# An encoder layer on one core: four of seven product sums moved into PSUM, operand pages freed one by one, second norm's statistics on ScalarE

## The chip, the cores and the metric

The kernel runs on one core of a Trainium2 chip. The metric is the device time of one execution in microseconds. The kernel before takes 1025.63 us (median of 3 runs, 1025.45 to 1026.38).

## The reference, cut to what matters

One layer of an encoder on 512 tokens of width 1024, in float32:

```
x = layer_norm(alpha*x + 0.5*swiglu_1(x))              # width 2816 in between
h = x @ w_in                                           # one projection, split into attention and conv parts
mix = concat([sparse_attention(h), short_conv(h)]) @ w_out
x = layer_norm(alpha*x + mix)                          # "second norm"
x = layer_norm(alpha*x + 0.5*swiglu_2(x))
x = x + sigmoid(x @ ple_gate_w) * (p @ ple_proj_w)     # "gate" and "embed"

swiglu(x, wg, wu, wd) = (silu(x @ wg) * (x @ wu)) @ wd
layer_norm(x) = (x - mean) * rsqrt(var + eps) * g + b  # over the 1024 columns of a token
```

## The kernel before, in words

The 512 tokens stand as four blocks of 128 (`nat[t]`), and transposed as operands. Every float32 matrix product is made of three passes on TensorE: an operand is split into a hi part (a cast on ScalarE, L111) and a lo part (a subtraction on VectorE, L112), and hi*hi, hi*lo and lo*hi are summed in PSUM (`mm`, L132). A recording layer with priorities sets the order of the instructions on each engine; each engine, and SP's queue of DMA issues, then works through its own list in that order.

On-chip memory is 38 pages of 4 KB per partition, handed out by `page` from a first-in first-out list and given back by `free`; the next user of a page waits for the last user of the one before. A load (`unit`, L114) takes three pages: raw, hi and lo, and gives raw back. PSUM has eight banks; `bank("all")` goes round them.

`ffn` (L244) goes through the 22 chunks of 128 of the middle width in groups of 4, 4, 4, 4 and 6. The first two chunks are plain products (`plain`). The other 20 go in ten pairs (`two`, L309): a pair of chunks by two halves of the tokens by two halves of the 1024 rows is a 2 by 2 block product, done with seven products in place of eight. `weights` (L276) loads the two halves of a pair's columns of wg or wu and makes the operands A11, A12/A22, S1/S2 and S3/S4 of them by additions on VectorE (L293, L294, L299, L300) and splits; `Quarters` makes the operands B and T of the tokens. One product is 2 matrices (g and u) x 4 x 3 = 24 matmuls of 256 columns, g in the left half of a bank and u in the right. Each product has a bank of its own, and `two` adds them up outside PSUM: one copy on ScalarE (L340), seven additions on VectorE (L341, 342, 344, 345, 347, 348, 349), into pages `e` (two) and `k` (two). `put_chunk` (L332) does silu on ScalarE (L336), the multiplication on VectorE (L337) and the split of the result. All of a pair's operand pages, `e` and `k` are given back at its end (L351). After each group comes the down projection (96 matmuls of 512 columns for four chunks) with the wd units, which are loaded as pages and priority allow; in the last group it goes block by block, with the layer norm (`ln_tb`, L156: aggregate L158, pow on GpSimd L160, two passes on VectorE L161 and L162) and the transposes (L146) of each block behind it.

Ahead of the second norm (L749 to L763) the output projection of block t is added to `nat[t]` (L757), `bn_stats` takes statistics on VectorE (L758), `ln_tb` follows, and `Quarters.block` transposes the block (L201), casts hi (L204), subtracts lo (L205) and copies raw (L224). The products `p @ ple_proj_w` (`embed`, L425) are made during the attention and around the second norm as filling work, copied to four pages (`prj`, L433) and held there until the gate at the very end (L785). The attention keeps its softmax rows in a ring of two tiles of 1280 columns (L686).

## Time and profile before

| | |
|---|---|
| median of 3 runs | 1025.63 us (1025.45 to 1026.38) |
| the profiled execution | 1025.29 us |
| its span | 1023.4 us |
| TensorE busy | 1004.4 us, 98% of the span |
| VectorE, ScalarE busy | 823.5 us (80%), 442.6 us (43%) |
| stages by the span | first feed-forward to about 330 us, first norm and combined projection, attention to about 600, second norm to about 630, second feed-forward to about 970, third norm and gate to the end |

The profiled execution takes 1.9 us more than its span, which lie before the first and behind the last instruction. An engine's busy time says how much of the span it worked; what it waited for stands in the timeline in square brackets, as the idle time just before an instruction and the instruction that released it. A wait of TensorE delays the end where TensorE has no idle time left to make up for it.

### The profile page before, as it was taken

How to read it: one execution, taken by the hardware profiler on the slowest of the kernel's cores; microseconds unless marked ns; L12 is line 12 of the kernel's file. 1: busy time of each engine (PE TensorE's matmuls, PEld its weight loads, DVE VectorE, ACT ScalarE, POOL GpSimd, SP SyncE). 2: the span in 40 equal slices, each digit the busy share in tenths (PEclk: the TensorE clock that was granted, in tenths of full speed). 3: DMA queues.
4: the chain of work that ended last, by engine and by line, in shares of the span. 5: the costliest groups of instructions: out<-in, count | busy, mean ns of one | idle time of the engine just before them, and what ended most of it. 6: DMA issues, size and time to landing. Idle time of an engine off the chain costs nothing.

```text
span 1023.4 us, 15531 instructions
## 1 busy us (share of the span) xinstructions
PE 1004.4 (98%) x6311; PEld 902.3 (88%) x6311; DVE 823.5 (80%) x1289; ACT 442.6 (43%) x627; POOL 27.0 (3%) x35
## 2 busy tenths in 40 slices
PE   9999999999999989999999999999999999999998
PEld 7989999898998868888878788989999898998787
DVE  7997868978698946999679988896868969698952
ACT  7544334433355225432576736443425324246221
POOL 1000000000002100000000011000000000000100
PEclk9999999999999999999999999999999999999999
DMA  9532324323226322423112222431324322236111
GB/s 306 162 109 83 104 83 145 101 80 113 79 100 200 83 61 62 120 67 84 61 42 103 83 71 94 128 120 45 120 84 144 103 79 89 82 124 226 56 38 51
DMA packets 99606, 104.57 MB, mean 102 GB/s; under 512 B 5968, under 2 KB 82000, under 8 KB 99536
## 3 DMA queue, kind: packets, MB, share of 16 engines
q1 hardware_dynamic: 99536, 103.60, 32.0%
q8 instruction: 49, 0.80, 0.3%
q14 instruction: 21, 0.17, 0.1%
HBM read 101.49 MB, written 2.10 MB: 101 GB/s over the span
## 4 chain that ended last, share of the span: by engine, by line
PE 87%; DVE 4%; DMA 4%; ACT 3%; issue 1%; SPq 1%; POOL 0%; POOLq 0%; ACTq 0%; DVEq 0%
PE bk L132 84%; DVE pg L112 2%; ACT pg L111 2%; DMA pg<-in_ffn_wd_dram 1%; PE bk L524 1%; DMA pg<-in_ffn_wu_dram 1%; PE bk L525 1%; PE bk L722 1%; PE bk L146 1%; DMA pg<-in_x_t_dram 1%; DMA pg<-in_ple_proj_w_dram 1%; ACT a L694 0%; SPq L214 0%; DMA pg<-in_ple_gate_w_dram 0%; DVE nat L162 0%
## 5 line engine op out<-in xcount | busy, mean ns | idle before, releaser
L132 PE MATMUL bk<-pg,pg 128*128 128x256 f32 (+1 forms) x2832 | 496.7, 333 | 4.9 <-DVE pg L112 2.1
L132 PEld LDWEIGHTS bk<-pg,pg 128*128 128x128 f32 x2832 | 427.3, 190 | 57.2 <-DVE pg L112 3.9
L111 ACT CAST pg<-pg 128x1024 fp32r<-128x1024 f32 (+1 forms) x270 | 260.0, 976 | 303.3 <-PE bk L132 76.0
L112 DVE TENSOR_TENSOR pg<-pg,pg 128x1024 fp32r<-128x1024 f32 (+1 forms) x270 | 301.1, 1126 | 38.3 <-ACT pg L111 33.0
L132 PE MATMUL bk<-xq,pg 128*128 128x256 f32 x2208 | 274.7, 284 | 2.2 <-DVE mv L158 1.4
L132 PEld LDWEIGHTS bk<-xq,pg 128*128 128x128 f32 x2208 | 269.4, 192 | 5.9 <-ACT pg L433 1.8
L132 PE MATMUL bk<-xT,pg 128*128 128x512 f32 (+2 forms) x600 | 133.0, 381 | 0.2 <-ACT xT L111 0.2
L132 PEld LDWEIGHTS bk<-xT,pg 128*128 128x128 f32 (+1 forms) x600 | 110.1, 186 | 21.2 <-ACT xT L111 0.5
L132 PE MATMUL bk<-pg,xT 128*128 128x512 f32 (+1 forms) x312 | 69.8, 374 | 2.0 <-DVE nat L394 1.7
L132 PEld LDWEIGHTS bk<-pg,xT 128*128 128x128 f32 x312 | 54.9, 188 | 12.2 <-ACT pg L111 2.1
L336 ACT ACTIVATE a<-pg 128x512 f32<-128x512 f32 x40 | 25.2, 630 | 78.0 <-DVE pg L345 70.8
L111 ACT CAST pg<-hf 128x512 fp32r<-128x512 f32 (+1 forms) x56 | 34.6, 618 | 37.6 <-DVE hf L337 19.3
L112 DVE TENSOR_TENSOR pg<-hf,pg 128x512 fp32r<-128x512 f32 (+1 forms) x56 | 38.7, 690 | 4.1 <-ACT pg L111 3.8
L408 DVE SCALAR_TENSOR_TENSOR nat<-bk,nat 128x512 f32<-128x512 f32 x64 | 40.3, 682 | 1.2 <-PE bk L132 1.2
L345 DVE TENSOR_TENSOR pg<-bk,pg 128x512 f32<-128x512 f32 x20 | 13.8, 691 | 29.3 <-PE bk L132 29.0
L337 DVE TENSOR_TENSOR hf<-a,pg 128x512 f32<-128x512 f32 x40 | 27.5, 688 | 11.8 <-ACT a L336 11.7
L160 POOL TENSOR_TENSOR mv<-mv,mhalf 128x1 f32<-128x1 f32 x12 | 17.8, 1479 | 630.4 <-DVE mv L159 630.4
L112 DVE TENSOR_TENSOR pg<-bk,pg 128x512 fp32r<-128x512 f32 (+2 forms) x37 | 22.5, 626 | 12.8 <-ACT pg L111 12.4
L293 DVE TENSOR_TENSOR pg<-pg,pg 128x512 f32<-128x512 f32 x40 | 27.3, 686 | 5.6 <-DMA pg<-in_ffn_wg_dram 5.0
L299 DVE TENSOR_TENSOR pg<-pg 128x512 f32<-128x512 f32 x40 | 27.4, 685 | 2.5 <-PE bk L132 2.5
L294 DVE TENSOR_TENSOR pg<-pg,pg 128x512 f32<-128x512 f32 x40 | 27.4, 684 | 0.0
L300 DVE TENSOR_TENSOR pg<-pg,pg 128x512 f32<-128x512 f32 x40 | 27.0, 685 | 0.1
(100 smaller groups left out, 614.5 us busy)
## 6 DMA issues: line engine op xcount, KB each, us to landing
pg<-in_ffn_wd_dram SPq DMA_DIRECT2D x44, 512.0 KB, 4.0
pg<-in_ffn_wu_dram SPq DMA_DIRECT2D x43, 512.0 KB, 4.8
pg<-in_ffn_wg_dram SPq DMA_DIRECT2D x43, 512.0 KB, 3.9
pg<-in_w_in_dram SPq DMA_DIRECT2D x28, 512.0 KB, 3.6
pg<-in_w_out_dram SPq DMA_DIRECT2D x8, 512.0 KB, 3.9
pg<-in_ple_gate_w_dram SPq DMA_DIRECT2D x8, 512.0 KB, 3.7
pg<-in_x_t_dram SPq DMA_DIRECT2D x8, 256.0 KB, 5.8
nat<-in_x_dram SPq DMA_DIRECT2D x4, 512.0 KB, 9.2
```

The costliest lines, as they stand in the source:

```text
L111: nc.scalar.copy(hi, src)
L112: nc.vector.tensor_sub(lo, src, hi.bitcast(F32))
L132: nc.tensor.matmul(ps, lhsT=st[a], rhs=mv[b], start=first and i == 0 and k == 0, stop=last and i == n - 1 and k == 2)
L160: nc.gpsimd.tensor_tensor(mv[:, 3:4], mv[:, 2:3], mhalf, op=ALU.pow)
L293: nc.vector.tensor_add(S1, A21, A22)
L294: nc.vector.tensor_sub(S2, S1, A11)
L299: nc.vector.tensor_sub(S3, A11, A21)
L300: nc.vector.tensor_sub(S4, A12, S2)
L336: nc.scalar.activation(s_t, e[m][:, :, 0], AF.Silu)
L337: nc.vector.tensor_mul(h3, s_t, e[m][:, :, 1])
L345: nc.vector.tensor_add(e[0][:, 1], prod("S4", "B22"), u4)
L408: nc.vector.scalar_tensor_tensor(dst, acc[t], CY, dst, op0=ALU.mult, op1=ALU.add)
```

## The change

It has these parts:

- In `two`, the seven products are taken in another order, and partial sums are kept in PSUM: A11B11, S2T2, S3T3 and A22T4 follow each other in one bank (`x_`), S1T1 and S4B22 in a second (`y_`), A12B21 has a third. The running sums are read out between: four copies on ScalarE (L365, 366, 367, 372) and three additions on VectorE (L368, 369, 370). The pages `k` are gone.
- In `weights`, the operands are made in the order in which the products take them (A11, S1/S2, S3/S4, A12/A22), and each operand's pages are given back with the last product that uses them; the pages of `e` are given back in `put_chunk` (L360).
- 40 pages in place of 38. The first warm-up tile lies in `nat[0]`.
- `prj` is stored to DRAM when it is made (L458) and loaded again for the gate (4 x 512 KB each way, on SP's queue).
- The softmax rows of a head lie in two pages (768 and 512 columns) in place of the ring.
- In the second norm, blocks 0 to 2 take their statistics on ScalarE: a pass for the sum, one for the sum of squares, each with an accumulator (`ln_tb_act`). Block 3 keeps `bn_stats`.

```diff
-NPAGES = 38
-WSTEPS = (1, 2, 1)
+NPAGES = 40
...
+    def ln_tb_act(r, g, b):
+        mv, junk = ring("mv", 4, [P, 4]), page([P, D], F32)
+        nc.scalar.activation(junk, r, AF.Identity, accum_out=mv[:, 0:1])
+        nc.vector.tensor_scalar(mv[:, 0:1], mv[:, 0:1], -1.0 / D, None, op0=ALU.mult)
+        nc.scalar.activation(junk, r, AF.Square, bias=mv[:, 0:1], accum_out=mv[:, 1:2])
+        free(junk)
+        nc.vector.tensor_scalar(mv[:, 2:3], mv[:, 1:2], 1.0 / D, LN_EPS / ALPHA ** 2, op0=ALU.mult, op1=ALU.add)
+        nc.gpsimd.tensor_tensor(mv[:, 3:4], mv[:, 2:3], mhalf, op=ALU.pow)
+        nc.vector.scalar_tensor_tensor(r, r, mv[:, 0:1], g, op0=ALU.add, op1=ALU.mult)
+        nc.vector.scalar_tensor_tensor(r, r, mv[:, 3:4], b, op0=ALU.mult, op1=ALU.add)
...
-            pages += [a11, *a2, *h12, *h34]
+            ops["S3"], ops["S4"] = (ops["S3"], h34), (ops["S4"], [])
+            yield
+            a2 = page([P, 4, 2 * P]), page([P, 4, 2 * P])
+            split(*a2, r[1])
+            free(r[1])
+            ops["A12"], ops["A22"] = (tuple(z[:, :, m * P:(m + 1) * P] for z in a2) for m in range(2))
+            ops["A12"], ops["A22"] = (ops["A12"], []), (ops["A22"], a2)
             yield
...
-            def prod(a, b):
-                ps = bank("all").rearrange("p (m n) -> p m n", m=2)
+            def product(ps, a, b, first):
                 for i, (nm, _) in enumerate(mats):
-                    mm(ps[:, i], [((W[nm][a][0][:, c], W[nm][a][1][:, c]), (X.q[b][0][:, c], X.q[b][1][:, c])) for c in range(4)])
+                    w = W[nm][a][0]
+                    for c in range(4):
+                        for k, (x_, y_) in enumerate(PASSES):
+                            nc.tensor.matmul(ps[:, i], lhsT=w[x_][:, c], rhs=X.q[b][y_][:, c],
+                                             start=first and i == 0 and c == 0 and k == 0,
+                                             stop=i == 1 and c == 3 and k == 2, skip_group_check=not first)
+                for nm, _ in mats:
+                    free(*W[nm][a][1])
                 return ps
...
-            nc.scalar.copy(p1, prod("A11", "B11"))
-            nc.vector.tensor_add(e[0][:, 0], prod("A12", "B21"), p1)
-            nc.vector.tensor_add(u2, prod("S2", "T2"), p1)
-            p5 = prod("S1", "T1")
-            nc.vector.tensor_add(u4, p5, u2)
-            nc.vector.tensor_add(e[0][:, 1], prod("S4", "B22"), u4)
+            x_, y_ = bank2(), bank2()
+            nc.scalar.copy(e[0][:, 0], product(x_, "A11", "B11", True))
+            nc.scalar.copy(e[1][:, 1], product(y_, "S1", "T1", True))
+            nc.scalar.copy(e[0][:, 1], product(x_, "S2", "T2", False))
+            nc.vector.tensor_add(e[0][:, 1], product(y_, "S4", "B22", False), e[0][:, 1])
+            nc.vector.tensor_add(e[1][:, 1], product(x_, "S3", "T3", False), e[1][:, 1])
+            nc.vector.tensor_add(e[0][:, 0], product(bank2(), "A12", "B21", True), e[0][:, 0])
             put_chunk(0)
-            nc.vector.tensor_add(u3, prod("S3", "T3"), u2)
-            nc.vector.tensor_add(e[1][:, 1], p5, u3)
-            nc.vector.tensor_add(e[1][:, 0], prod("A22", "T4"), u3)
+            nc.scalar.copy(e[1][:, 0], product(x_, "A22", "T4", False))
             put_chunk(1)
-            free(*pages, *e, *k)
             return h
...
+                prj.append(dp.tile([P, 1024], F32, tag=f"prj{t}", name=f"prj{t}"))
+                nc.sync.dma_start(prj[t], pr)
+                free(pr)
...
+            if t == NTB - 1:
+                nc.vector.bn_stats(stats[:, half], dst)
+        if t == NTB - 1:
+            ln_tb(nat[t], stats, g_t, b_t)
+        else:
+            ln_tb_act(nat[t], g_t, b_t)
```

How it moves instructions is seen at two places. In the rows below a name is a tile (`pg` a page, `bk` a bank, `nat` a token block, `xq` an operand of the tokens) with its running number, and what an instruction waits for stands at the row's end.

The first place is ScalarE's list in the first feed-forward, around the change from one pair to the next in a group. Before:

```order
L111 CAST pg_320_2978<-pg_315_2963 128x1024 [waits DVE_49,PE_49]
L340 COPY pg_324_2984<-bk_2986 128x512 [waits PE_49]
L336 ACTIVATE a_2926<-pg_295_2732 128x512 [waits DVE_49]
L111 CAST pg_329_3185<-pg_328_3183 128x1024 [waits DMAHW4_49]
L111 CAST pg_336_3200<-pg_334_3196 128x512 [waits DMAHW5_49,Activation_49]
L111 CAST pg_299_2929<-hf_2925 128x512 [waits DVE_49]
```

Now:

```order
L372 COPY pg_281_2684<-bk_2685 128x512 [waits PE_49]
L358 ACTIVATE a_2871<-pg_281_2684 128x512 [waits Activation_49]
L111 CAST pg_283_2874<-hf_2870 128x512 [waits DVE_49]
L111 CAST pg_311_3123<-pg_310_3121 128x1024 [waits DMAHW4_49]
L365 COPY pg_306_2927<-bk_2929 128x512 [waits PE_49]
L111 CAST pg_325_3153<-pg_323_3149 128x1024
L111 CAST pg_315_3131<-pg_313_3127 128x512 [waits DMAHW5_49,Activation_49]
L366 COPY pg_307_2928<-bk_2930 128x512 [waits PE_49]
L111 CAST pg_321_3145<-pg_319_3141 128x1024 [waits DVE_49]
L367 COPY pg_306_2927<-bk_2929 128x512 [waits PE_49]
```

The copy of the new pair's first product (L340 before, L365 now) stood ahead of the cast of a wd unit that waits for its transfer (`DMAHW4`), and stands behind it now; three more copies follow in the pair.

The second place is VectorE's list at the second norm, from the two passes over block 3 on. Before:

```order
L161 SCALAR_TENSOR_TENSOR nat_71<-nat_71,mv_6016,pg_546_5790 128x1024
L205 TENSOR_TENSOR pg_564_5967<-bk_5968,pg_563_5966 128x4x128 [waits Activation_49]
L205 TENSOR_TENSOR xq_2_5819<-bk_5976,xq_2_5818 128x4x128 [waits Activation_49]
L162 SCALAR_TENSOR_TENSOR nat_71<-nat_71,mv_6016,pg_547_5792 128x1024 [waits DVE_49,Pool_49]
L205 TENSOR_TENSOR pg_564_5967<-bk_6022,pg_563_5966 128x4x128 [waits Activation_49]
L205 TENSOR_TENSOR xq_2_5819<-bk_6029,xq_2_5818 128x4x128 [waits Activation_49]
```

Now, directly behind L162 of block 3:

```order
L302 TENSOR_TENSOR pg_595_6294<-pg_589_6280,pg_590_6282 128x512 [waits PE_49]
L310 TENSOR_TENSOR pg_596_6295<-pg_589_6280 128x512
L303 TENSOR_TENSOR pg_595_6294<-pg_595_6294,pg_589_6280 128x512 [waits DVE_49]
L302 TENSOR_TENSOR pg_599_6302<-pg_592_6287,pg_593_6289 128x512 [waits DMAHW2_49,DMAHW0_49,PE_49]
L309 TENSOR_TENSOR pg_596_6295<-pg_590_6282,pg_595_6294 128x512 [waits DVE_49]
L112 TENSOR_TENSOR pg_598_6299<-pg_595_6294,pg_597_6298 128x1024 [waits Activation_49]
L303 TENSOR_TENSOR pg_599_6302<-pg_599_6302,pg_592_6287 128x512 [waits DVE_49]
L310 TENSOR_TENSOR pg_600_6303<-pg_592_6287 128x512 [waits PE_49]
L112 TENSOR_TENSOR pg_594_6291<-pg_592_6287,pg_594_6291 128x512 [waits DMAHW3_49,Activation_49]
L112 TENSOR_TENSOR pg_602_6307<-pg_599_6302,pg_601_6306 128x1024 [waits Activation_49]
L309 TENSOR_TENSOR pg_600_6303<-pg_593_6289,pg_599_6302 128x512
L217 TENSOR_TENSOR pg_563_5913<-bk_5968,pg_562_5912 128x4x128 [waits PE_49]
```

Block 3's low parts (L205 before, L217 now) stood directly behind its last pass; now eleven operations on the weights of the second feed-forward's first pair stand between.

## Rows read from the trace of the kernel before

**Rows 1.** Page, part 1: busy time of each engine, share, instructions.

```profile
PE 1004.4 (98%) x6311; PEld 902.3 (88%) x6311; DVE 823.5 (80%) x1289; ACT 442.6 (43%) x627; POOL 27.0 (3%) x35
```

**Rows 2.** Stretches: length, busy us (instructions) PE, PEld, DVE, ACT, POOL; clock; DMA share; GB/s.

```profile
200.00:220.00 20.00, 20.00 (x169) 20.00 (x169) 13.17 (x19) 6.17 (x9) 0.00 (x0) 1.00 0.13 40
320.00:340.00 20.00, 18.12 (x81) 14.30 (x80) 18.57 (x26) 8.04 (x10) 5.73 (x3) 1.00 0.48 148
340.00:380.00 40.00, 36.99 (x176) 28.73 (x175) 27.13 (x39) 9.83 (x15) 4.57 (x3) 1.00 0.25 66
500.00:600.00 100.00, 96.97 (x491) 79.26 (x490) 78.81 (x201) 70.45 (x147) 0.00 (x0) 1.00 0.23 74
600.00:620.00 20.00, 17.28 (x85) 13.61 (x84) 19.02 (x31) 7.44 (x13) 2.91 (x2) 1.00 0.09 26
920.00:1000.00 80.00, 78.50 (x423) 66.53 (x422) 60.84 (x81) 27.85 (x35) 5.82 (x4) 1.00 0.31 106
```

**Rows 3.** Timeline in one pair: start us, us, engine, line, tiles, [idle before, releaser].

```profile
206.05 5.92 PE L132 MATMUL bk<-xq,pg 128*128 128x256 f32 x48
...
211.81 5.92 PE L132 MATMUL bk<-pg,pg 128*128 128x256 f32 x48
212.01 0.69 DVE L345 TENSOR_TENSOR pg<-bk,pg 128x512 f32<-128x512 f32 x1 [2.19 <-PE bk L132]
212.74 0.63 ACT L336 ACTIVATE a<-pg 128x512 f32<-128x512 f32 x1 [6.21 <-DVE pg L345]
213.40 0.69 DVE L337 TENSOR_TENSOR hf<-a,pg 128x512 f32<-128x512 f32 x1 [0.70 <-ACT a L336]
```

**Rows 4.** Lines by shape: busy us, mean ns of one, idle before and releasers.

```profile
L112 DVE TENSOR_TENSOR pg<-pg,pg 128x1024 fp32r<-128x1024 f32 x223 | 269.8, 1219 | 36.0 <-ACT pg L111 31.2 <-ACT a L336 2.7 <-PE bk L132 1.6
L111 ACT CAST pg<-pg 128x1024 fp32r<-128x1024 f32 x223 | 232.1, 1051 | 265.9 <-PE bk L132 62.1 <-DMA pg<-in_ffn_wd_dram 48.2 <-DVE pg L294 46.2
L342 DVE TENSOR_TENSOR pg<-bk,pg 128x512 f32<-128x512 f32 x20 | 13.8, 690 | 15.4 <-PE bk L132 14.8
L340 ACT COPY pg<-bk 128x512 f32<-128x512 f32 x20 | 11.7, 585 | 13.6 <-PE bk L132 12.7 <-DVE pg L112 1.0
L694 ACT ACTIVATION_READ_ACCUMULATOR a<-a,ss 128x1 f32 x32 | 6.0, 187 | 0.0
```

**Rows 5.** Page, part 6: issues, KB each, us from issue to landing.

```profile
pg<-in_ffn_wd_dram SPq DMA_DIRECT2D x44, 512.0 KB, 4.0
pg<-in_ffn_wu_dram SPq DMA_DIRECT2D x43, 512.0 KB, 4.8
```

**Rows 6.** Timeline at the end of the first feed-forward.

```profile
323.55 1.04 ACT L111 CAST pg<-pg 128x1024 fp32r<-128x1024 f32 x1 [3.25 <-DMA pg<-in_ffn_wd_dram]
...
324.65 5.54 PE L132 MATMUL bk<-pg,pg 128*128 128x512 f32 x23 [1.07 <-ACT pg L111]
...
331.00 3.24 PE L132 MATMUL bk<-pg,pg 128*128 128x512 f32 x13 [0.81 <-DVE pg L112]
```

**Rows 7.** Timeline from the first norm into the combined projection.

```profile
359.89 5.69 PE L132 MATMUL bk<-pg,xT 128*128 128x512 f32 x24 [1.70 <-DVE nat L394]
...
366.36 1.06 PE L146 MATMUL bk<-ident,nat 128*128 128x128 f32 x8 [0.78 <-DVE nat L162]
```

**Rows 8.** Timeline around the second norm.

```profile
608.58 1.03 PE L201 MATMUL bk<-ident,nat 128*128 128x128 f32 x8
...
616.31 1.67 PE L132 MATMUL bk<-pg,pg 128*128 128x512 f32 x6 [0.78 <-DVE nat L757]
...
619.41 4.07 PE L132 MATMUL bk<-xq,pg 128*128 128x256 f32 x32 [1.43 <-DVE mv L158]
...
628.76 4.49 PE L132 MATMUL bk<-pg,pg 128*128 128x512 f32 x30
```

**Rows 9.** Timeline at the end of the second feed-forward and in the third norm.

```profile
940.24 5.13 PE L132 MATMUL bk<-pg,pg 128*128 128x512 f32 x21 [0.24 <-DVE pg L112]
...
970.08 1.06 PE L146 MATMUL bk<-ident,nat 128*128 128x128 f32 x8 [0.56 <-DVE nat L162]
```

More of the change, by code (lines that the diff above doesn't have):

```diff
@@ L68, in layer_kernel @@
     pp = ctx.enter_context(tc.tile_pool(name="pp", bufs=1, space=bass.MemoryType.PSUM))
+    dp = ctx.enter_context(tc.tile_pool(name="dp", bufs=1, space=bass.MemoryType.DRAM))
     x, out = x[0], out[0]
@@ L274, in plain, with weights @@
             return put(hf)
-        def weights(w, fc, ops, pages):
+        def weights(w, fc, ops):
             r = []
@@ L284, in weights @@
             split(a11[:, 0], a11[:, 1], A11)
-            ops["A11"] = a11[:, 0], a11[:, 1]
-            yield
-            a2 = page([P, 4, 2 * P]), page([P, 4, 2 * P])
-            split(*a2, r[1])
-            ops["A12"], ops["A22"] = (tuple(z[:, :, m * P:(m + 1) * P] for z in a2) for m in range(2))
+            ops["A11"] = (a11[:, 0], a11[:, 1]), [a11]
             yield
@@ L305, in weights, with bank2 @@
             ops["S3"], ops["S4"] = (tuple(z[:, i] for z in h34) for i in range(2))
-            pages += [a11, *a2, *h12, *h34]
+            ops["S3"], ops["S4"] = (ops["S3"], h34), (ops["S4"], [])
[5 more added lines that the diff above has]
+            ops["A12"], ops["A22"] = (ops["A12"], []), (ops["A22"], a2)
             yield
         def two(fc, ah):
-            W, pages = {nm: {} for nm, _ in mats}, []
-            steps = [weights(w, fc, W[nm], pages) for nm, w in mats]
+            W = {nm: {} for nm, _ in mats}
+            steps = [weights(w, fc, W[nm]) for nm, w in mats]
             with tc.high_priority(offset=ah):
-                for n in WSTEPS:
+                for _ in range(4):
                     for g in steps:
-                        for _ in range(n):
-                            next(g)
-            def prod(a, b):
-                ps = bank("all").rearrange("p (m n) -> p m n", m=2)
+                        next(g)
+            def bank2():
+                return bank("all").rearrange("p (m n) -> p m n", m=2)
+            def product(ps, a, b, first):
                 for i, (nm, _) in enumerate(mats):
-                    mm(ps[:, i], [((W[nm][a][0][:, c], W[nm][a][1][:, c]), (X.q[b][0][:, c], X.q[b][1][:, c])) for c in range(4)])
+                    w = W[nm][a][0]
[6 more added lines that the diff above has]
+                    free(*W[nm][a][1])
                 return ps
             e = [page([P, 2, 2, 256], F32) for _ in range(2)]
-            k = [page([P, 2, 2, 256], F32) for _ in range(2)]
-            p1, u2, u3, u4 = k[0][:, 0], k[0][:, 1], k[1][:, 0], k[1][:, 1]
             h = []
@@ L425, in embed @@
     def embed(t):
-        prj.append(page([P, 1024], F32))
+        pr = page([P, 1024], F32)
         for half in range(2):
@@ L432, in embed @@
                      (wp[c][0][:, 0, hs], wp[c][1][:, 0, hs])) for c in range(2)])
-            nc.scalar.copy(prj[t][:, hs], ps)
+            nc.scalar.copy(pr[:, hs], ps)
+            if half:
+                prj.append(dp.tile([P, 1024], F32, tag=f"prj{t}", name=f"prj{t}"))
+                nc.sync.dma_start(prj[t], pr)
+                free(pr)
             yield
     first = {}
-    warm = sb.tile([P, 512], F32, name="warm")
+    warm = nat[0][:, :512]
     nc.vector.memset(warm, 0.0)
@@ L685, in softmax @@
         slope = 2.0 ** -(h + 1)
-        a = soft[h] = ring("a", 2, [P, 1280])
+        sp = [page([P, 768], F32), page([P, 512], F32)]
+        a = [sp[t // 3][:, TOFF[t % 3]:TOFF[t % 3] + (t + 1) * P] for t in range(NTB)]
+        soft[h] = a, sp
         st = ring("ss", 2, [P, NTB, 3])
@@ L709, in av @@
                 for t in range(b, NTB):
[L710 removed]
+                    nc.tensor.transpose(ps[:, n:n + P], a[t][:, b * P:(b + 1) * P], ident)
                     n += P
@@ L716, in av @@
                 pT[b] = both(pg, slice(at[b], at[b] + (NTB - b) * P))
+        free(*sp)
         pull(fill)
@@ L775, in layer_kernel @@
     for t in range(NTB):
+        pr = page([P, 1024], F32)
+        with tc.high_priority(offset=AHEAD_G):
+            nc.sync.dma_start(pr, prj[t])
         for half in range(2):
@@ L784, in layer_kernel @@
                 nc.scalar.activation(sg[:, :n], ps[:, :n], AF.Sigmoid)
-                nc.vector.tensor_mul(sg[:, :n], sg[:, :n], prj[t][:, hs])
+                nc.vector.tensor_mul(sg[:, :n], sg[:, :n], pr[:, hs])
                 ot = ring("hf", 2, [P, 512])
@@ L788, in layer_kernel @@
                 nc.sync.dma_start(out[ts(t), hs], ot[:, :n])
+        free(pr)
 _INS = ["x", "ln1_g", "ln1_b", "ffn1_wg", "ffn1_wu", "ffn1_wd", "w_in", "conv_w", "w_out", "ln2_g", "ln2_b",
```

17 lines of the change are left out of this document (8 added, 9 removed).

## The prediction

> **What bounds the kernel now.** I read the totals first, then the stages, then the waits of each stage. TensorE is busy 1004.4 of 1023.4 us [rows 1], so all idle time of it together is 19 us: nothing that another engine saves counts unless TensorE waited for it. The table by stretches [rows 2] says where that is: inside the two feed-forward stages it is busy 20.00 of 20.00 us at a granted clock of 1.00 (the 2.4 GHz level), at the end of the first and in the norm behind it 1.88 and 3.01 us are lost (320 to 340 and 340 to 380 us), in the attention 3.03 (500 to 600), around the second norm 2.72 (600 to 620), at the end 1.50 (920 to 1000). The matmuls themselves are the same 6311 in number and size after the change, so the change can only move these waits, or make new ones.
>
> In the feed-forward stage a product is 24 matmuls: 48 of them take 211.81 - 206.05 = 5.76 us [rows 3], so 0.120 us each, 2.88 us a product and 20.16 us a pair. VectorE works 13.17 and ScalarE 6.17 of 20 us there [rows 2]. The reader is to see in [rows 3] that the drain of a product begins 0.20 us behind the next product's start (212.01 against 211.81), and that silu and multiply follow in 0.63 and 0.69 us, each some 0.04 later.
>
> **The change, part by part.**
>
> *Fewer drains.* Per pair three VectorE additions of 0.69 us are left of seven, and ScalarE has four copies of 0.585 instead of one [rows 4]. Over 20 pairs that takes 80 x 0.69 = 55 us from VectorE and puts 60 x 0.585 = 35 us on ScalarE. Neither ends last in a stretch where TensorE is busy 20.00 of 20.00, so I cost both at nothing; the cover is gone only if a drain is late, which is the next part.
>
> *One bank, several products.* Before, each product has its own of eight banks, and a drain may be late by several products. Now S2T2 goes on in the bank of A11B11, S4B22 in that of S1T1, S3T3 and A22T4 again in the first: each must wait until the copy of the bank's last state is done, and only one product lies between. Slack: 2.88 - 0.20 - 0.585 = 2.1 us. One cast of 1.05 us [rows 4] ahead of the copy in ScalarE's queue fits; one that itself waits for a transfer may not. The order shows such a cast: in the second pair of a group the hi part of a down-projection unit stands directly ahead of the copy L365. Its raw page is a page of e that is free with L359 of the pair before. With the first pair's start as zero: A12B21 ends at 6 x 2.88 = 17.28, its addition L370 at 17.28 + 0.20 + 0.69 = 18.17, silu at 18.84, L359 at 19.56, or 20.1 if one weight operation stands ahead; the transfer lands 4.0 us later [rows 5], at 23.6 to 24.1; cast 1.05 and copy 0.585 end at 25.2 to 25.8, with four handings-on at 0.04 each 25.4 to 26.0. TensorE wants the bank at 20.16 + 5.76 = 25.92. So this is a matter of tenths: margin 0.5 to a miss of 0.1; with the 4.8 us that the up weights' transfers take [rows 5], a miss of 0.9. There are 10 such pairs (three groups of two and one of three in each feed-forward). Bounds 0 and 10 x 0.9 = 9 us (below zero nothing, since the stage is full); I take 0.25 each, **+2.5**, because the row for exactly this transfer is the 4.0, and transfers scatter about it.
>
> *Pages back with the last product.* In the last pair of the first feed-forward the cast of a late wd unit waited 3.25 us for the landing (323.55), and TensorE stood 1.07 and then 0.81 us [rows 6]. Now the pages of S3/S4, S1/S2 and A11 come back inside the pair; the last two units take pages that the pair's first and third product give back, so they start at least four products, 11.5 us, ahead of the down projection, against 4.0 + 1.05 + 1.22 = 6.3 needed [rows 4, 5]. The 1.88 goes, less some 0.3 for the last chunk's silu: **-1.6**. What is late next is the norm: behind it stand waits such as 1.70 and 0.78 [rows 7], where low parts of w_in (1.23 us each, gated by transfers) lie between the last block's norm operations on VectorE. Two of four are earlier now; of the 3.0 us in 340 to 380 I take **-0.8**, bounds -3.0 and +1.2 (one more low part in between). In the second feed-forward the wd and gate loads come forward in the same way; of the 1.50 us lost in 920 to 1000 [rows 2] (0.24 at 940 us by wd's lo part, 0.56 at 970 us by the norm's last instruction, [rows 9]) I take **-1.0**, bounds -1.5 and 0.
>
> *prj through DRAM.* Four stores and four loads of 512 KB on SP's queue. The loads are wanted only by the gate's multiplication, and issued tens of microseconds ahead against 4.0 to 4.8 us for a load of this size [rows 5]: nothing; without that cover it would be one landing, 4 us. Softmax in pages instead of a ring takes 2 x 2 pages of the 4 that prj no longer holds and 2 that are new: even, zero, bounds -1.5 and +2 on the 3.0 us of the attention stage.
>
> *Second norm.* For three blocks two passes of ScalarE, 1.05 us each by the casts of this size [rows 4] and an accumulator read of 0.19 [rows 4], replace the two VectorE passes of statistics over half a block, about 0.69 us each like L342, of which one lies on the chain: 2 x 1.24 - 0.69, some 1.8 us longer, while VectorE gets 3 x 2 x 0.69 = 4.1 us back in a stretch where it is busy 19.02 of 20 [rows 2]. These two about cancel: followed through the new lists with these durations, block 0's transposes come 2.5 us later than 608.58 [rows 8], block 1's 0.7 earlier, blocks 2 and 3 where they were. But behind block 3's L162 the order now puts eleven weight operations ahead of its low parts L217: nine of 0.69 and two of 1.22 us [rows 4], 8.6 us, one of them also behind the store of the last prj. TensorE has the transposes, 1.03 us, and 33 matmuls, 4.0 us, until it needs the first L217, which ends at 8.6 + 0.7 = 9.3: it stands 4.3 us. Before, block 3's low parts stood directly behind its L162 and TensorE went on without a wait (30 matmuls from 628.76, [rows 8]). Against that, 6 matmuls of 512 columns (5.54 / 23 = 0.24 us each, [rows 6]) and 5 of 256, 2.0 us, now run before those transposes and not behind them, in waits that were empty, such as the 0.78 and 1.43 [rows 8]. **+2.3**, bounds -0.7 and +4.3.
>
> **Load or order at the second norm.** VectorE is busy 19.02 of 20 us just where TensorE loses 2.72 [rows 2], and both of the larger waits are on VectorE (L757, L158, [rows 8]). If its load sets them, the 4.1 us taken off it clear them, and the second norm gives -2.7 in place of +2.3, the sum 5.0 less. I keep the walk, since the new wait is one of queue order, which less load does not mend. The Trainium skill ("Perfetto Trace Analysis", section "Optimizing Scalar/DVE Operations") speaks for the load: where DVE is saturated, work may be better off on Scalar; by it the -2.7 would stand.
>
> **Sum.** +2.5 - 1.6 - 0.8 - 1.0 + 0 + 2.3 = +1.4 us on the profiled execution's 1025.29, of which 1.9 lie outside the span; that run stands 0.34 below the median of 1025.63, so 1027.0.
>
> **The rivals.**
> - *All margins hold* (faster). Copies come in time (0 instead of +2.5), and the eleven weight operations find cover or the freed VectorE carries block 3 forward (0 instead of +2.3): -3.4, 1022.2 (chance 0.20); if load sets the waits at the second norm, another 2.7 off, 1019.5 (chance 0.12). For it: ScalarE is idle two thirds of the time in the full stage. Against: the order of its queue.
> - *Banks wait for copies* (slower). The same cast ahead of L365, with landings at 4.8 us or one more cast before it: 0.9 to 1.1 us at 10 pairs, +9 to 11 instead of +2.5, so 1033.5 to 1035.5. It decides as soon as the landing takes over 4.1 us from L359's end. For it: the row of wd is a median, and loads of the next pair share the queue. Against it: no row of before shows a copy that late. The Trainium skill ("Perfetto Trace Analysis", section "Matmul Optimizations") wants all 8 PSUM banks used; three serve a pair here, and by that rule this rival wins; no row of before shows a shared bank.
> - *It does not do what it says*: the pages come no earlier because SP's queue is in order and an earlier load holds it up. Then the -1.6 and -1.0 are missing: 1029.6.
>
> **How the numbers follow.** Forecast 0.38 (within 4 us of 1027.0), all margins hold 0.32, banks wait 0.17, pages no earlier 0.08, something outside 0.05. A run can tell 0.2%, 2.05 us, from no change, so same is 1023.6 to 1027.7. Of the forecast 0.21 lie there, 0.15 above, 0.02 below; of the faster rival 0.04 lie inside and 0.28 below; the third rival has 0.03 inside. Faster 0.02 + 0.28 + 0.03 = 0.33, same 0.28, slower 0.15 + 0.17 + 0.05 + 0.02 = 0.39. The likeliest case alone spans 1023 to 1031; the range goes on to the faster rival's 1019.0 and the slower one's 1035.5.
>
> **What would show it.** Right: no TensorE wait at 324 us; waits on ScalarE's L365 or L366, tenths of a microsecond, once in a second pair; one wait of about 4 us behind block 3's transposes, released by L217. Wrong: full stretches of 20.00 everywhere in the feed-forward stages with the second norm free of waits (the faster rival), or waits of a microsecond on L365 at all ten pairs.

## The result, and the profile after

The changed kernel takes 1035.44 us (median of 6 runs, 1032.27 to 1039.2), the kernel before, run beside it, 1025.61 us: a ratio of 1.0091, 95% interval 1.0077 to 1.0106, so 9.3 us slower (7.9 to 10.9). The forecast was 1027.0, the range 1019.0 to 1035.5. The profiled execution of after took 1032.27 us with a span of 1030.4: 7.0 us more than before in the span.

The totals moved the way the prediction had them, by less (it had 55 us off VectorE and 35 onto ScalarE for the feed-forward pairs alone): TensorE has the same 6311 matmuls, VectorE has lost some 45 us and ScalarE gained 30 [rows 1]. Page of after, part 1 (busy time of each engine, share, instructions):

```profile
PE 1006.8 (98%) x6311; PEld 904.0 (88%) x6311; DVE 778.0 (76%) x1203; ACT 472.8 (46%) x699; POOL 25.2 (2%) x35
```

The stretches of after that answer to [rows 2] (length, busy us and instructions of PE, PEld, DVE, ACT, POOL, granted clock, DMA share, GB/s):

```profile
200.00:220.00 20.00, 20.00 (x169) 20.00 (x168) 17.27 (x22) 12.92 (x18) 0.00 (x0) 1.00 0.51 154
320.00:340.00 20.00, 15.78 (x79) 12.48 (x77) 14.80 (x24) 6.92 (x11) 6.46 (x5) 1.00 0.26 79
340.00:380.00 40.00, 37.89 (x177) 29.57 (x175) 27.77 (x39) 9.41 (x14) 4.57 (x3) 1.00 0.29 79
500.00:600.00 100.00, 94.99 (x479) 78.17 (x478) 77.06 (x199) 72.26 (x150) 0.00 (x0) 0.98 0.25 85
600.00:620.00 20.00, 19.76 (x95) 16.00 (x95) 16.34 (x24) 10.56 (x19) 2.71 (x2) 1.00 0.29 85
620.00:650.00 30.00, 27.49 (x200) 25.20 (x199) 28.74 (x38) 22.88 (x33) 2.91 (x2) 1.00 0.47 155
920.00:1000.00 80.00, 78.36 (x450) 67.82 (x449) 54.09 (x71) 25.73 (x36) 5.74 (x4) 1.00 0.31 112
```

and one of before that was not shown, for the second half of the second norm:

```profile
620.00:650.00 30.00, 29.78 (x239) 29.02 (x238) 26.88 (x33) 17.17 (x24) 2.91 (x2) 1.00 0.27 88
```

TensorE's busy time fell from 18.12 to 15.78 at the end of the first feed-forward, from 96.97 to 94.99 in the attention (with the clock at 0.98 there), and from 29.78 to 27.49 behind the second norm; it rose from 17.28 to 19.76 in 600 to 620.

Busy time hides small gaps and the clock, so I also take the **lost time** of TensorE: for each matmul the distance to the next one's start, less what a matmul of its width takes undisturbed in this trace (0.227 us for 512 columns, 0.173 for 384, 0.120 for 256, 0.063 for 128). Up to 1000 us it sums to 38.6 us before and 45.5 after, and the difference is the 7.0 of the spans. By stage, in us, for the kernels that the text below speaks of (columns by label; stretches in us of the span; a stop counts where the next matmul starts):

```
                              before  after   e3   e6   e5  e12   e9  e10
0-20     start                   5.7    5.6  5.7  6.0  5.6  5.6  5.5  5.5
20-320   first feed-forward      0.2    1.7  2.6  0.8  0.6  0.2  2.6  0.0
320-350  its end                 3.3    6.4  5.8  3.6  3.6  2.8  3.8  3.0
350-380  first norm              5.1    3.5  3.8  5.5  5.6  5.7  5.1  5.3
380-500  projection, attention   1.9    1.9  2.1  2.0  2.0  1.9  2.0  1.8
500-590  attention              11.8    9.1  9.6 11.9 11.8 11.9 11.7 12.2
590-600  its end                 0.7    6.0  6.4  1.5  0.9  0.7  0.9  1.2
600-630  second norm             5.6    2.1  2.3  3.3  5.7  5.8  5.3  3.6
630-660  behind it               0.0    4.2  1.3  1.7  0.4  0.0  0.9  0.2
660-920  second feed-forward     0.0    0.6  0.7  0.2  0.0  0.0  0.1  0.7
920-1000 end, third norm, gate   4.3    4.4  4.6  4.9  5.4  4.8  8.4  4.6
```

Where after differs, the timelines (start us, us, engine, line, tiles, [idle before, releaser]) say why.

**Shared banks, as predicted.** At 222 us, in a second pair, the cast of a wd unit waits for its transfer, the copy L365 stands behind it, and TensorE waits for the copy:

```profile
222.32 1.05 ACT L111 CAST pg<-pg 128x1024 fp32r<-128x1024 f32 x1 [1.95 <-DMA pg<-in_ffn_wd_dram]
...
223.28 0.58 ACT L365 COPY pg<-bk 128x512 f32<-128x512 f32 x1
...
223.91 0.38 PE L343 MATMUL bk<-pg,pg 128*128 128x256 f32 x1 [0.45 <-ACT pg L365]
```

The two full stretches lose 1.5 + 0.6 = 2.1 us more than before, in five places where a bank is written again and its reader is late. Three of the readers are copies on ScalarE (L365 here, L367 at 313 us, L366 at 725); two are the addition L369 on VectorE, at 298 us (there behind low parts) and at 671.

**End of the first feed-forward.** The wait for wd of [rows 6] is gone; this came in its place:

```profile
319.31 1.05 ACT L111 CAST pg<-pg 128x1024 fp32r<-128x1024 f32 x1 [1.14 <-DMA pg<-in_w_in_dram]
320.26 0.63 ACT L358 ACTIVATE a<-pg 128x512 f32<-128x512 f32 x1
...
325.04 0.56 DVE L582 TENSOR_TENSOR dm<-dm,a 128x384 f32<-128x384 f32 x1 [1.06 <-POOL a L581]
325.51 0.68 DVE L359 TENSOR_TENSOR hf<-a,pg 128x512 f32<-128x512 f32 x1
326.23 0.62 ACT L111 CAST pg<-hf 128x512 fp32r<-128x512 f32 x1 [2.22 <-DVE hf L359]
...
326.90 0.73 PE L132 MATMUL bk<-pg,pg 128*128 128x512 f32 x2 [1.86 <-ACT pg L111]
...
339.14 0.87 PE L146 MATMUL bk<-ident,nat 128*128 128x128 f32 x6 [1.75 <-DVE nat L162]
```

With pages back early, w_in's first loads come ahead of the last pair's end, and their cast (319.31) waits 1.14 us for a transfer in front of the silu of that pair's first chunk (320.26). The multiplication of the last chunk (L359 at 325.51) then stands behind a mask operation (L582) that waits 1.06 for GpSimd; the chunk's cast follows, and TensorE stands 1.86 us. Block 0's norm is late in its turn: its transposes (L146, 339.14) wait 1.75 us for L162. The norm behind loses less (3.5 in place of 5.1), its end more (6.4 in place of 3.3).

**End of the attention.** The largest place. SP's queue, two of its waits (what waited <- for what: us, times, longest), and the two instructions that it decides:

```profile
581.11 0.33 SPq L458 DMA_DIRECT2D prj<-pg  x1
583.00 0.33 SPq L118 DMA_DIRECT2D pg<-in_w_out_dram  x1
584.21 0.38 SPq L118 DMA_DIRECT2D pg<-in_ffn_wg_dram  x1
584.64 0.57 SPq L118 DMA_DIRECT2D pg<-in_w_out_dram  x1
```

```profile
SPq L118 <- PE bk L751: 1.6, 1, 1.6
SPq L118 <- PE bk L738: 1.0, 1, 1.0
```

```profile
590.43 1.04 ACT L111 CAST pg<-pg 128x1024 fp32r<-128x1024 f32 x1 [0.36 <-DMA pg<-in_w_out_dram]
...
591.53 0.73 PE L132 MATMUL bk<-pg,pg 128*128 128x512 f32 x2 [3.49 <-ACT pg L111]
```

```profile
580.00:590.00 10.00, 8.04 (x44) 6.34 (x42) 9.88 (x28) 9.90 (x22) 0.00 (x0) 1.00 0.61 211
590.00:592.00 2.00, 0.47 (x2) 0.30 (x2) 1.68 (x4) 1.60 (x3) 0.00 (x0) 1.00 0.09 24
592.00:594.00 2.00, 2.00 (x10) 1.77 (x9) 2.00 (x4) 0.00 (x0) 0.00 (x0) 0.71 1.11 361
594.00:596.00 2.00, 2.00 (x6) 1.50 (x6) 0.40 (x2) 0.95 (x2) 0.00 (x0) 0.50 0.34 139
596.00:598.00 2.00, 2.00 (x15) 1.82 (x14) 0.79 (x2) 1.60 (x3) 0.00 (x0) 0.94 0.00 0
```

The last load of w_out goes out only at 584.64 us (580.46 before). It waits for the landing of the store of prj's first block (581.11), but that store had landed at 583.73. What held it longer is the queue: the load of w_out ahead of it (583.00) took a page that the attention's last products (L751) had used, and the load of wg (584.21) one that the transposes of the softmax rows (L738) had read. The last load lands at 590.4, its cast ends at 591.5, and TensorE has stood 3.49 us. Then the granted clock is 0.71, 0.50 and 0.94 in three stretches of 2 us: TensorE runs at 1.2 GHz for part of them, and a matmul of 512 columns starts every 0.427 us there and not every 0.227. Half of the time at that level is lost, (0.29 + 0.50 + 0.06) x 2 = 1.7 of the 5.3 us which 590 to 600 loses more than before. The attention ahead of it loses 2.7 less, so from 500 to 600 us 2.6 of the 7.0 are lost.

**Second norm.** Less is lost ahead of block 3 (5.6 to 2.1), and behind its transposes the weights that now stand ahead of its low parts:

```profile
636.47 0.62 ACT L111 CAST pg<-pg 128x512 fp32r<-128x512 f32 x1 [0.94 <-DMA prj<-pg]
...
637.14 0.50 PE L343 MATMUL bk<-xq,pg 128*128 128x256 f32 x2 [0.58 <-ACT pg L111]
...
638.65 1.45 PE L343 MATMUL bk<-xq,pg 128*128 128x256 f32 x10 [1.00 <-DVE pg L112]
...
640.25 0.68 DVE L217 TENSOR_TENSOR pg<-bk,pg 128x512 fp32r<-128x512 f32 x1
...
640.99 0.39 PE L132 MATMUL bk<-pg,pg 128*128 128x256 f32 x1 [0.89 <-DVE pg L217]
```

Three waits of 0.58, 1.00 and 0.89 us: the first behind a cast whose page is freed by the store of prj, the second released by a low part of the weights (L112), the last by L217.

The median execution lies 3.2 us above the profiled one, and in part the granted clock goes with it: its mean is 0.998 in the profiled execution and 0.993 to 0.995 in four of the other five. At 1.2 GHz half of the time is lost, so 0.0035 less clock on 1030 us is some 3.6 us (an estimate). It is not the whole of it: the fifth took 1035.34 us at 0.998.

### The profile page after: what moved, and what is told of

It is laid out like the page before. It is cut to its first block, busy times and chain, and to the rows that moved or that the text cites. A ratio compares the mean times of both kernels' runs of the same rounds, so it can differ in the third digit from the quotient of the medians.

```text
span 1030.4 us, 15411 instructions
## 1 busy us (share of the span) xinstructions
PE 1006.8 (98%) x6311; PEld 904.0 (88%) x6311; DVE 778.0 (76%) x1203; ACT 472.8 (46%) x699; POOL 25.2 (2%) x35
## 4 chain that ended last, share of the span: by engine, by line
PE 80%; DVE 8%; DMA 6%; ACT 3%; POOL 1%; issue 1%; SPq 1%; POOLq 0%; DVEq 0%; ACTq 0%
PE bk L132 43%; PE bk L343 33%; DVE pg L112 3%; DMA pg<-in_ffn_wd_dram 2%; ACT pg L111 2%; DMA pg<-in_w_out_dram 1%; POOL mv L160 1%; DVE nat L162 1%; PE bk L550 1%; DMA pg<-in_w_in_dram 1%; PE bk L146 1%; DMA pg<-in_ple_gate_w_dram 1%; PE bk L551 1%; PE bk L751 1%; DMA pg<-in_x_t_dram 1%
## 5 line engine op out<-in xcount | busy, mean ns | idle before, releaser
L111 ACT CAST pg<-pg 128x1024 fp32r<-128x1024 f32 (+1 forms) x270 | 256.7, 975 | 276.0 <-PE bk L132 137.2
L112 DVE TENSOR_TENSOR pg<-pg,pg 128x1024 fp32r<-128x1024 f32 (+1 forms) x270 | 300.0, 1127 | 71.7 <-ACT pg L111 57.3
L132 PE MATMUL bk<-pg,pg 128*128 128x512 f32 (+1 forms) x1392 | 319.2, 385 | 7.3 <-ACT pg L111 5.4
L343 PE MATMUL bk<-xq,pg 128*128 128x256 f32 x1920 | 241.3, 283 | 1.8 <-DVE pg L112 1.0
L343 PE MATMUL bk<-pg,pg 128*128 128x256 f32 x1440 | 182.9, 283 | 0.7 <-ACT pg L365 0.4
L302 DVE TENSOR_TENSOR pg<-pg,pg 128x512 f32<-128x512 f32 x40 | 27.4, 686 | 59.2 <-DMA pg<-in_ffn_wg_dram 59.2
L112 DVE TENSOR_TENSOR pg<-hf,pg 128x512 fp32r<-128x512 f32 (+1 forms) x56 | 38.3, 684 | 8.1 <-ACT pg L111 7.9
L132 PE MATMUL bk<-xq,pg 128*128 128x256 f32 x288 | 37.6, 287 | 0.9 <-ACT xq L111 0.6
L359 DVE TENSOR_TENSOR hf<-a,pg 128x512 f32<-128x512 f32 x40 | 27.5, 689 | 13.8 <-ACT a L358 13.2
L112 DVE TENSOR_TENSOR pg<-bk,pg 128x512 fp32r<-128x512 f32 (+2 forms) x37 | 22.6, 625 | 12.8 <-ACT pg L111 12.6
L111 ACT CAST xT<-bk 128x512 fp32r<-128x512 f32 x16 | 8.6, 590 | 49.2 <-PE bk L146 49.2
```

Source lines behind the costliest of these rows:

```text
L111: nc.scalar.copy(hi, src)
L112: nc.vector.tensor_sub(lo, src, hi.bitcast(F32))
L132: nc.tensor.matmul(ps, lhsT=st[a], rhs=mv[b], start=first and i == 0 and k == 0, stop=last and i == n - 1 and k == 2)
L302: nc.vector.tensor_add(S1, A21, A22)
L343: nc.tensor.matmul(ps[:, i], lhsT=w[x_][:, c], rhs=X.q[b][y_][:, c], start=first and i == 0 and c == 0 and k == 0, stop=i == 1 and c == 3 ...
L359: nc.vector.tensor_mul(h3, s_t, e[m][:, :, 1])
```

## The experiments

Two theories stood at the start. *Page trade*: the new use of pages makes loads late at the end of the attention and stretches of weight work early elsewhere, and a stop of TensorE then takes the clock with it. Its rival, *shared banks*: three banks in place of seven make TensorE wait for copies. Ratios are to the kernel before, run beside each; differences of two kernels combine the half-widths of their intervals by the root of the sum of squares, and 0.001 is 1.03 us.

**e1, e2: the store taken out of the way.** In e1 the pages of the first two prj blocks are given back only after the w_out loads have theirs; in e2 prj stays on the chip.

```diff
-                free(pr)
+                late.append(pr)
...
     wo = [unit(rows(w_out, c * P, 1), [P, 1, 1024], AHEAD_O2) for c in range(4)]
+    free(*late)
```

> Edit: the pages of the first two prj blocks are given back only when the four w_out units have their pages, so no w_out load waits for a store. Theory 'store chain' (the 3.5 us stop of TensorE at 591 us comes from a w_out load whose page is free only when the store of prj has landed, and the stop makes the clock fall behind it): the stop goes, granted clock 1.000 in every run, 1026 to 1028 us, 8 under the changed kernel's 1035.4. Rival 'shared banks' (the loss sits in the feed-forward waits for copies): 1034 to 1036, as before this edit. Rival 'clock by itself' (the clock falls whatever the stop): about 1031, clock still 0.993 to 0.998.

```diff
-                prj.append(dp.tile([P, 1024], F32, tag=f"prj{t}", name=f"prj{t}"))
-                nc.sync.dma_start(prj[t], pr)
-                free(pr)
+                prj.append(pr)
...
-        pr = page([P, 1024], F32)
-        with tc.high_priority(offset=AHEAD_G):
-            nc.sync.dma_start(pr, prj[t])
+        pr = prj[t]
```

> Edit: prj stays in its four pages, no store and no load. Store chain: stop at 591 us gone as in e1, and the 0.6 us wait behind the store of the last prj at 637 us too: 1025.5 to 1027.5 us, clock 1.000. But four pages fewer in the second feed-forward: if these loads then come late (rival 'pages'), TensorE waits of 1 to 2 us at some down projections, 1029 to 1033. Shared banks: 1034 to 1036.

Measured: e1 1034.42 us, ratio 1.0084 (1.0068 to 1.0099); e2 1033.65, 1.0071 (1.0058 to 1.0084). Both miss what was expected: at best 2 us come back. e1 did not take the store out of the way: a load of wg, which stands ahead of the last w_out load in SP's queue, now waited 3.4 us for it (the queue's waits in e1), and the w_out load went out at 586.35, later than in after. The one stop became four of 0.33 to 1.24 us, ending at 588.0 to 591.6 us, with the same low clock. e2 has no store at all, and there the last w_out load still goes out only at 584.5 us: its page was last used by the transposes of the softmax rows (L736, the queue's waits in e2):

```profile
SPq L118 <- PE bk L736: 2.9, 1, 2.9
```

So the store is not what makes this load late. TensorE stops there in e2 for one more reason (timeline and stretches):

```profile
588.74 1.04 ACT L111 CAST pg<-pg 128x1024 fp32r<-128x1024 f32 x1
...
589.67 0.59 ACT L455 COPY pg<-bk 128x512 f32<-128x512 f32 x1
...
590.31 1.22 PE L132 MATMUL bk<-pg,pg 128*128 128x512 f32 x2 [2.22 <-ACT pg L455]
```

```profile
580.00:590.00 10.00, 7.23 (x38) 5.36 (x37) 9.87 (x28) 9.90 (x23) 0.00 (x0) 0.97 0.32 105
590.00:592.00 2.00, 1.69 (x4) 1.40 (x5) 1.86 (x5) 0.26 (x1) 0.00 (x0) 0.50 0.20 52
592.00:594.00 2.00, 2.00 (x8) 1.61 (x8) 0.67 (x1) 0.00 (x0) 0.00 (x0) 0.50 0.70 210
```

TensorE waits 2.22 us for a copy (L455) that stands in ScalarE's queue behind a w_out cast; ScalarE is busy 9.90 of 10 us ahead of it, in after as well. So the theory became: the softmax rows in pages are what crowds this place, by late loads or by ScalarE's queue. Elsewhere e2 loses 0.4 us in place of 4.2 behind block 3, and gives it back as its rival 'pages' had it: 3.6 in place of 0.6 in the second feed-forward and 6.0 in place of 4.4 at its end.

**e3: block 3 ahead of the weight operations.**

```diff
-        X.copies(X.block(t, "all"))
+        with tc.high_priority(offset=600 if t == NTB - 1 else 0):
+            X.copies(X.block(t, "all"))
```

> Edit: the transposes and splits of the second norm's block 3 get a higher priority, so three weight operations stand ahead of its L217 in place of eleven. If the 4.2 us lost at 630 to 642 us come from that order: the waits at 637, 638.6 and 641 us go, 3 to 4 us less, 1031.5 to 1032.5 us; the stop at 591 us and the lower clock stay. If they come from the store of the last prj: at most 1 us less, 1034.5.

Measured: 1032.54 us, 1.0057 (1.0044 to 1.0069), so 3.5 us less than after (1.5 to 5.4). The loss in 630 to 660 goes from 4.2 to 1.3, the stop at 590 stays. The queue order behind block 3 is a cause, as the prediction's walk through the lists had it.

**e4: a bank for each product, in the change.**

```diff
-            nc.scalar.copy(e[1][:, 1], product(y_, "S1", "T1", True))
-            nc.scalar.copy(e[0][:, 1], product(x_, "S2", "T2", False))
+            p5 = prod("S1", "T1")
+            nc.vector.tensor_add(u2, prod("S2", "T2"), p1)
+            nc.vector.tensor_add(u4, p5, u2)
...
```

> Edit: each of the seven products has a bank of its own again, with one copy and seven additions as before the change; order of products, pages and all else as in the changed kernel. Store chain: only the 1.8 us of waits in the feed-forward stages can go, 1033.5 to 1035.5 us; VectorE's 55 us more are hidden. Shared banks: 1027 to 1029.

Measured: 1034.26 us, 1.0074 (1.0061 to 1.0088), 1.7 less than after (-0.3 to 3.7). The feed-forward stretches lose nothing any more, but the additions take two more of the 40 pages, and 630 to 660 loses 8.1 us in place of 4.2, with the clock low at 640 to 647. In the change the shared banks are not what costs 9 us.

**e6: the softmax ring again.**

```diff
-NPAGES = 40
+NPAGES = 38
...
-        sp = [page([P, 768], F32), page([P, 512], F32)]
-        a = [sp[t // 3][:, TOFF[t % 3]:TOFF[t % 3] + (t + 1) * P] for t in range(NTB)]
-        soft[h] = a, sp
+        ar = ring("a", 2, [P, 1280])
+        a = [ar[:, TOFF[t]:TOFF[t] + (t + 1) * P] for t in range(NTB)]
+        soft[h] = a, ()
```

> The change with the softmax rows in a ring of two buffers again and 38 pages, all else as in the change (prj through DRAM too). Theory 'attention's pages': the last load of w_out no longer waits for the store of prj, TensorE's 3.5 us stop at 591 us and the half clock behind it (together some 5 us) go: 1028 to 1031. Rival 'any stop elsewhere drops the clock' (the stops at 326, 339 and 637 to 641 us set it): the clock's mean stays at 0.994 to 0.996 and the time at 1033 to 1036.

Measured: 1028.85 us, 1.0018 (1.0008 to 1.0028): 7.5 us less than after (5.7 to 9.3), with the store of prj, ScalarE's statistics and the shared banks all still there. The page trade, that is softmax in pages together with 40 pages, is the larger part of the loss. The last w_out load now goes out by 581.7 us, its cast is done five microseconds earlier, and the clock holds (SP's queue, timeline, stretches of e6):

```profile
574.49 7.18 SPq L118 DMA_DIRECT2D pg<-in_w_out_dram  x2
581.72 0.43 SPq L458 DMA_DIRECT2D prj<-pg  x1
```

```profile
585.64 1.06 ACT L111 CAST pg<-pg 128x1024 fp32r<-128x1024 f32 x1 [0.73 <-DMA pg<-in_w_out_dram]
...
589.30 0.50 PE L751 MATMUL bk<-pg,pg 128*128 128x512 f32 x1 [0.94 <-ACT pg L111]
```

```profile
580.00:590.00 10.00, 8.92 (x48) 7.26 (x47) 9.14 (x29) 9.05 (x22) 0.00 (x0) 1.00 0.54 157
590.00:592.00 2.00, 2.00 (x11) 1.60 (x10) 2.00 (x3) 1.45 (x3) 0.00 (x0) 1.00 0.00 0
592.00:594.00 2.00, 2.00 (x11) 1.65 (x10) 2.00 (x4) 0.00 (x0) 0.00 (x0) 1.00 0.65 262
```

The table shows that the ring also gives back the 2.8 us lost more at the first feed-forward's end, though the first norm then loses 2.0 more, and 2.5 of the 4.2 us behind block 3. That fewer loads run ahead with 38 pages is a likely reason for both, not shown. Ring and page count were changed together, and softmax in pages with 38 pages was not run, so their shares stay open. The profiled executions show 4.0 of the 7.5 us (spans of 1030.4 and 1026.4); the mean clock of all executions, 0.9953 in after and 0.9985 in e6, would make some 3.3 more by the working above (an estimate).

**e5, e9, e12: the feed-forward part alone**, put into the kernel before: as in the change (e5); with the pages kept to the pair's end (e9); with the pages early and a bank for each product (e12).

```diff
-                    free(*W[nm][a][1])
+                    held.extend(W[nm][a][1])
...
             put_chunk(1)
+            free(*held, *e)
```

> The kernel of before with the new feed-forward pair alone (three banks for seven products, pages back with their last product); prj in pages, 38 pages, softmax ring and VectorE statistics as before. Theory 'attention's pages and the clock' (the loss comes from the 3.5 us stop of TensorE at 591 us and the half clock behind it): no stop there and a granted clock of 1.0 in 590 to 600; the shared banks cost their 1.8 us, the end of FFN1 about as much as in the change, so 1025 to 1029 us. Rival 'shared banks': the feed-forward part carries the loss, 1032 to 1036.

> The feed-forward part alone once more, but all pages of a pair back at its end as before, so that of this part only the shared banks are left. Theory 'early pages bring new stops' (w_in's casts come early and stand ahead of the last chunk's silu, TensorE's 0.5 to 0.7 us stops at 324 to 328 us): those go, the 1.2 us stop of before at 324 us comes back, the clock stays at 1.0; 1026 to 1029 beside 1027 of before and 1031 of the feed-forward part alone. Rival 'shared banks': as the feed-forward part alone, 1030 to 1033.

> The feed-forward part alone (fifth run) with a bank of its own for each product and the additions on VectorE, so that of the part its order of products and weight steps and the early pages are left. If shared banks carry the loss of the feed-forward part: as before, 1026 to 1028. If the order does (the last chunk's silu follows later behind the last products, the stops of 0.5 to 2 us at 324 to 331 and 944 to 947 us that both runs with this part show): 1030 to 1032.

Measured: e5 1031.03 us, 1.0037 (1.0021 to 1.0053); e9 1031.07, 1.0040 (1.0027 to 1.0054); e12 1026.37, 0.9992 (0.9980 to 1.0004). With before itself this is a table of two by two: own banks give no change that shows, pages late or early; shared banks cost some 4 us in both. e5 less e12 is 4.6 us (2.6 to 6.7). e5 came out above what was expected, e9 by its rival, and e12 as its first reading had it: here, without the page trade, the shared banks are the whole loss. That counts them with their readers, since e12 also puts one copy and seven additions back in place of four copies and three additions; sharing and the work moved to ScalarE were not run apart. In e9 one of them costs 1.71 us at once: a copy (L354) behind a cast that waited 2.53 us for wd (timeline):

```profile
40.04 1.04 ACT L111 CAST pg<-pg 128x1024 fp32r<-128x1024 f32 x1 [2.53 <-DMA pg<-in_ffn_wd_dram]
...
40.99 0.58 ACT L354 COPY pg<-bk 128x512 f32<-128x512 f32 x1
...
41.62 0.62 PE L331 MATMUL bk<-xq,pg 128*128 128x256 f32 x3 [1.71 <-ACT pg L354]
```

In e12 the same late cast of wd does nothing, since TensorE goes on in another bank:

```profile
222.63 1.05 ACT L111 CAST pg<-pg 128x1024 fp32r<-128x1024 f32 x1 [0.90 <-DMA pg<-in_ffn_wd_dram]
...
223.29 2.92 PE L331 MATMUL bk<-pg,pg 128*128 128x256 f32 x23
```

The profiled executions show 2.3 of the 4.6 us (1026.6 against 1024.3 span): 0.4 in the full stretch, 0.8 at the first feed-forward's end, 0.6 at the second's and in the norm behind it. Of the other half 0.4 lie outside the span (2.2 us there in e5, 1.8 in e12), and the mean clock of all executions, 0.9981 against 0.9991, would make some 1.0 (an estimate); the rest is not located. The 8.4 us of e9 at 920 to 1000 hold a fall of the clock to 0.53 and 0.62 at 948 to 952.

The parts do not add up: 7.5 us for the page trade and 4.6 for the banks are more than the 9.3 of the change, in which the banks alone were worth 1.7 (e4). What e6 has beyond e5, prj through DRAM and ScalarE's statistics, does not cost: e6 is 2.0 us shorter (0.0 to 3.9).

**e7, e8: the mask's scratch out of the ring.** e7 is e6 with block 3 ahead as in e3 and this edit, e8 is e5 with this edit:

```diff
-        dn = ring("a", 2, [P, 512])
+        dn = page([P, 512], F32)
...
+        free(dn)
```

> As the run before (ring, 38 pages), and block 3's normalization ahead of the weight operations at the second norm, and the mask's scratch in a page of its own and not in the ring that a GpSimd operation holds at the end of FFN1. Theory 'attention's pages, and small stops each worth themselves': 5 us less by the ring, 3 less by block 3, up to 1.5 less by the scratch: 1023 to 1027, the clock at 1.0. Rival 'stops move on': waits of 1 to 2 us turn up elsewhere, 1029 to 1033.

> The feed-forward part alone, as two runs before, with the mask's scratch in a page of its own. If VectorE's wait for GpSimd between the two silu multiplications of the last chunk sets the stop at 327 us: 1 to 1.5 us less than the feed-forward part alone. If the late casts on ScalarE set it: no difference that shows (within 1 us).

Measured: e7 1031.00 us, 1.0036 (1.0024 to 1.0048), 1.8 above e6; e8 1032.48, 1.0047 (1.0033 to 1.0061), not below e5. The edit does what it should (320 to 330 us loses 0.8 in place of 2.3 in e7, 1.4 in place of 2.3 in e8), and the first norm loses it again: 6.9 in place of 5.5, and 8.2 in place of 5.6. The other edit of e7, block 3 ahead, gives nothing there: 630 to 660 loses 1.7 us with it and, in e6, without it. "Stops move on" is right here. In e8 the clock falls there, behind two stops in a row (timeline of TensorE):

```profile
367.74 1.06 PE L146 MATMUL bk<-ident,nat 128*128 128x128 f32 x8 [1.34 <-DVE nat L162]
...
370.80 2.07 PE L132 MATMUL bk<-pg,xT 128*128 128x512 f32 x4 [1.31 <-DVE xT L112]
```

**e10, e11: the second norm's statistics alone**, put into the kernel before; in e11 with block 3 ahead as in e3.

```diff
-            nc.vector.bn_stats(stats[:, half], dst)
-        ln_tb(nat[t], stats, g_t, b_t)
+            if t == NTB - 1:
+                nc.vector.bn_stats(stats[:, half], dst)
+        if t == NTB - 1:
+            ln_tb(nat[t], stats, g_t, b_t)
+        else:
+            ln_tb_act(nat[t], g_t, b_t)
```

> The kernel of before with the second norm's statistics of three blocks on ScalarE alone. By the prediction's term +2.3 beside before. By the rival that VectorE's load sets the waits -2.7. By the two traces (600 to 630 us 3.5 less, 630 to 642 us 4.2 more, of which the order of weight operations in this kernel, without the early pages, may keep a part) -1 to +1.

> As the run before, with block 3's normalization placed ahead of the weight operations. If the stops of 637 to 641 us were of order alone: 1.5 to 3.5 us less than before (1023.5 to 1025.5 beside 1027). If ScalarE's two passes themselves are late: no gain over before (within 1 us).

Measured: e10 1025.84 us, 0.9995 (0.9983 to 1.0006); e11 1025.88, 0.9990 (0.9980 to 1.0001). Neither can be told from before. In the stretches of e10, beside 17.28 in [rows 2] and 29.78 above:

```profile
600.00:620.00 20.00, 19.89 (x110) 16.91 (x109) 18.04 (x26) 13.78 (x24) 4.36 (x3) 1.00 0.19 53
620.00:650.00 30.00, 28.79 (x228) 27.86 (x228) 26.70 (x35) 19.56 (x28) 1.46 (x1) 1.00 0.34 98
```

the second norm gains 2.6 us of TensorE's time in its first half and gives back 1.0 in its second. The 4.2 us behind block 3 do not appear; with the early pages but 38 of them (e6) 1.7 is lost there, so they come with the change's 40 pages, softmax pages or both. No version that was run beats the kernel before by more than can be measured.

## Why the prediction was right or wrong

**The size was wrong**: 1027.0 stood for no change that can be told, and 1035.44 is slower by 9.3 us, at the upper end of the range; of the three chances, slower had the largest, 0.39. That this is the time given for "banks wait for copies" (1033.5 to 1035.5) bears out nothing: in the change those waits cost 2.1 us, not 9 to 11, and it is luck that the range reached so far for that reason.

- **Softmax in pages instead of a ring: the step that failed.** It counted pages ("even, zero", bounds -1.5 and +2). Measured by e6 the trade, with its 40 pages, costs 7.5 us (5.7 to 9.3). The count was not what mattered: a page is back only when its last user is done. Loads now take pages of the softmax rows, which come back with the transposes that read them (L738 in after, L736 in e2), and the last load of w_out goes out 4 us later than before. That it also waits for a store of prj is not what decides: without any store (e2) it goes out at 584.5. The same paragraph's other half, prj through DRAM for nothing, is not contradicted (e6 beside e5). And the attention did gain (500 to 590 loses 2.7 less), which brought TensorE earlier to the place where ScalarE is busy 9.90 of 10 us and w_out is missing.
- **One bank, several products, +2.5**: the mechanism was right, a bank whose reader is late, and the full stretches lose 2.1 us. But that the sizes agree is in part luck: of five waits one has the form that was priced at ten pairs (wd's cast ahead of L365 in a second pair), and two are on VectorE's L369, which was not considered. Alone, by e5 and e12, it is 4.6 us (2.6 to 6.7) with the readers' move; 0.8 of them is lost at the first feed-forward's end. The Trainium skill ("Perfetto Trace Analysis", section "Matmul Optimizations") wants all 8 PSUM banks used; these two runs agree with it, with 4.6 us for three banks and their readers in place of one bank for each product.
- **Pages back with the last product, -1.6, -0.8, -1.0**: the wait for wd is gone, as predicted, and nothing is gained. In after 320 to 380 us lose 9.9 in place of 8.4, and in e12, with own banks, 8.5. "Less some 0.3 for the last chunk's silu" was the weak term: that chain became the wait, at 1.86 us. The end of the second feed-forward gave 0 in place of -1.0.
- **Second norm, +2.3**: the walk named the right waits, and e3 confirms the order as the cause (3.5 us). It had one wait of 4.3 us on L217; there are three, of 0.58, 1.00 and 0.89 us, only the last on L217, and 630 to 660 loses 4.2 us in all. It underrated the gain ahead of block 3 (3.5 us in place of 2.0); in place it is 2.1 + 4.2 - 5.6 = +0.7. The rival "load" is not borne out as -2.7: ScalarE's statistics alone are worth 0.5 us, between 1.7 less and 0.6 more. The Trainium skill ("Perfetto Trace Analysis", section "Optimizing Scalar/DVE Operations") says that moving work off a saturated VectorE may make sense; here that gains nothing that can be measured.
- **The clock** was in no term. The prediction had 1.00 everywhere and priced each wait at its own length.
